# Softmax over 32,768 logits: loads and stores in units of 4 MB instead of 1 MB, with six large buffers and coarser compute pieces

## Chip, cores, metric

One core of one Trainium2 chip (trn2). The metric is the device time of one execution in microseconds (us). The median of the kernel before was 2552.28 us over 5 runs (2549.58 to 2561.99). The kernel before varied by half a per cent from run to run.

## The reference

```python
logits = np.random.randn(16, 256, 32768).astype(np.float32);  temperature = 1.0
scaled = logits / temperature
scaled = scaled - scaled.max(axis=-1, keepdims=True)
e = np.exp(scaled)
return e / e.sum(axis=-1, keepdims=True)
```

The input is 536.9 MB and so is the output: 1,073.7 MB have to cross between HBM (the large memory) and SBUF (the on-chip memory).

## The kernel before

Each row of 32,768 values is split in two halves, so the data becomes 8,192 rows of 16,384 values. A tile is 128 such rows (8.4 MB), and there are 64 tiles. Every piece of 2,048 columns is loaded, gets its own maximum (on DVE, the vector engine) and its own exponential and sum (on ACT, the scalar engine), and stays on chip. SP issues the loads and POOL (GpSimd) the stores; the DMA engines move the data. When all eight pieces of a tile are through, the local maxima and sums are combined into one factor per piece. Then every piece is scaled in place and stored.

```python
C = 2048                                    # columns of one piece; 8 KB per partition row
XBUFS = min((190 * 1024) // (C * 4), 4 * NCH)          # 23 buffers of 1 MB
...
for t in range(n_tiles):
    for c in range(NCH):                                # NCH = 8
        xc = xpool.tile([P, C], fp32, tag="x", name="xc")
        nc.sync.dma_start(out=xc[:rp], in_=x[r0:r1, bass.ts(c, C)])      # load, SP queue
        nc.vector.tensor_reduce(out=nm[:rp, c : c + 1], in_=xc[:rp], ..., op=A.max, negate=True)
        nc.scalar.activation(out=xc[:rp], in_=xc[:rp], func=Exp, bias=nm[:rp, c : c + 1],
                             scale=inv_t, accum_out=ssum[:rp, c : c + 1])
    with tc.high_priority():
        ...   # combine maxima (nM), ee = exp(nm - nM), S = sum(ee * ssum), f = ee / S
    for c in range(NCH):
        if scale_on_act(c):                             # c % 8 not in (1, 4, 7)
            nc.scalar.activation(out=xc[:rp], in_=xc[:rp], func=Copy, scale=f[:rp, c : c + 1])
        else:
            nc.vector.tensor_scalar_mul(out=xc[:rp], in0=xc[:rp], scalar1=f[:rp, c : c + 1])
        nc.gpsimd.dma_start(out=o[r0:r1, bass.ts(c, C)], in_=xc[:rp])    # store, POOL queue
```

The order of the instructions on each engine is not the order of this text: a scheduler fixes it when the kernel is built.

Of the kernel before, what the change touches and what calls it, by code (L numbers as in the profile page):

```python
# [1 line left out]

# [4 lines left out]


@with_exitstack  # L10
def kernel(
    ctx: ExitStack,
    tc: tile.TileContext,
    logits: bass.AP,
    temperature: bass.AP,
    out: bass.AP,
):
    nc = tc.nc

    inv_t = 1.0 / float(temperature)  # L20

    P = nc.NUM_PARTITIONS
    xf = logits.flatten_outer_dims()
    of = out.flatten_outer_dims()
    N, V = xf.shape

    SPLIT = 2 if (V % 2 == 0 and (N * 2) % P == 0) else 1
    C = 2048
    while (V // SPLIT) % C != 0:
        C //= 2  # L30
    x = xf.rearrange("n (h v) -> (n h) v", h=SPLIT) if SPLIT > 1 else xf
    o = of.rearrange("n (h v) -> (n h) v", h=SPLIT) if SPLIT > 1 else of
    NR, VR = x.shape
    NCH = VR // C
    n_tiles = (NR + P - 1) // P

    XBUFS = min((190 * 1024) // (C * 4), 4 * NCH)

    def scale_on_act(c: int) -> bool:
        return (c % 8) not in (1, 4, 7)  # L40

    xpool = ctx.enter_context(tc.tile_pool(name="x", bufs=XBUFS))
    spool = ctx.enter_context(tc.tile_pool(name="stats", bufs=4))

    fp32 = mybir.dt.float32
    Exp = mybir.ActivationFunctionType.Exp
    Copy = mybir.ActivationFunctionType.Copy
    X = mybir.AxisListType.X
    A = mybir.AluOpType

    swap_mask = [i ^ 1 for i in range(32)]

    for t in range(n_tiles):
        r0 = t * P
        r1 = min(r0 + P, NR)
        rp = r1 - r0

        nm = spool.tile([P, NCH], fp32, tag="nm", name="nm")
        ssum = spool.tile([P, NCH], fp32, tag="ssum", name="ssum")
        ee = spool.tile([P, NCH], fp32, tag="ee", name="ee")  # L60
        f = spool.tile([P, NCH], fp32, tag="f", name="f")
        ttj = spool.tile([P, NCH], fp32, tag="ttj", name="ttj")
        nMh = spool.tile([P, 1], fp32, tag="nMh", name="nMh")
        nMp = spool.tile([P, 1], fp32, tag="nMp", name="nMp")
        nM = spool.tile([P, 1], fp32, tag="nM", name="nM")
        Sh = spool.tile([P, 2], fp32, tag="Sh", name="Sh")
        Sp = spool.tile([P, 1], fp32, tag="Sp", name="Sp")
        rS = spool.tile([P, 1], fp32, tag="rS", name="rS")

        chunks = []  # L70
        for c in range(NCH):
            xc = xpool.tile([P, C], fp32, tag="x", name="xc")
            chunks.append(xc)
            nc.sync.dma_start(out=xc[:rp], in_=x[r0:r1, bass.ts(c, C)])  # L74
            nc.vector.tensor_reduce(  # L75
                out=nm[:rp, c : c + 1],
                in_=xc[:rp],
                axis=X,
                op=A.max,
                negate=True,  # L80
            )
            if inv_t != 1.0:
                nc.vector.tensor_scalar_mul(
                    out=nm[:rp, c : c + 1], in0=nm[:rp, c : c + 1], scalar1=inv_t
                )
            nc.scalar.activation(  # L86
                out=xc[:rp],
                in_=xc[:rp],
                func=Exp,
                bias=nm[:rp, c : c + 1],  # L90
                scale=inv_t,
                accum_out=ssum[:rp, c : c + 1],
            )

        with tc.high_priority():
            nc.vector.tensor_reduce(out=nMh[:rp], in_=nm[:rp], axis=X, op=A.min)  # L96
            if SPLIT == 2:
                nc.vector.stream_shuffle(out=nMp[:rp], in_=nMh[:rp], mask=swap_mask)  # L98
                nc.vector.tensor_tensor(  # L99
                    out=nM[:rp], in0=nMh[:rp], in1=nMp[:rp], op=A.min  # L100
                )
            else:
                nM = nMh
            nc.scalar.activation(  # L104
                out=ee[:rp], in_=nm[:rp], func=Exp, bias=nM[:rp], scale=-1.0
            )
            nc.vector.tensor_tensor_reduce(  # L107
                out=ttj[:rp],
                in0=ee[:rp],
                in1=ssum[:rp],  # L110
                scale=1.0,
                scalar=0.0,
                op0=A.mult,
                op1=A.add,
                accum_out=Sh[:rp, 0:1],
            )
            if SPLIT == 2:
                nc.vector.stream_shuffle(  # L118
                    out=Sh[:rp, 1:2], in_=Sh[:rp, 0:1], mask=swap_mask
                )  # L120
                nc.vector.tensor_tensor(  # L121
                    out=Sp[:rp], in0=Sh[:rp, 0:1], in1=Sh[:rp, 1:2], op=A.add
                )
            else:
                Sp = Sh[:, 0:1]
            nc.vector.reciprocal(out=rS[:rp], in_=Sp[:rp])  # L126
            nc.scalar.activation(  # L127
                out=f[:rp], in_=ee[:rp], func=Copy, scale=rS[:rp]
            )

        for c in range(NCH):
            xc = chunks[c]
            if scale_on_act(c):
                nc.scalar.activation(  # L134
                    out=xc[:rp], in_=xc[:rp], func=Copy, scale=f[:rp, c : c + 1]
                )
            else:
                nc.vector.tensor_scalar_mul(  # L138
                    out=xc[:rp], in0=xc[:rp], scalar1=f[:rp, c : c + 1]
                )  # L140
            nc.gpsimd.dma_start(out=o[r0:r1, bass.ts(c, C)], in_=xc[:rp])  # L141


# [1 line left out]
_INS = ['logits', 'temperature']  # L145
_OUTS = [((16, 256, 32768), 'float32')]
#: Inputs that are plain numbers.
_NUMBERS = {'temperature': 1.0}


# [26 lines left out]
```

## Time and profile before

| | before |
|---|---|
| median time | 2552.28 us |
| profiled span | 2554.0 us |
| busy: DMA / ACT / DVE | over 90% / 65% / 57% |
| rate in an undisturbed slice | 427 to 428 GB/s, read and written together |
| 1,073.7 MB at 427.5 GB/s | 2,512 us |

First, lines of the page of before. In part 2 each digit or number stands for one of 40 equal slices of the span (64 us each): the busy share of the DMA engines in tenths, and what they moved. Part 3 has one line per DMA queue (q1 carries the loads, q0 the stores): packets, MB, and the time their packets took as a share of 16 engines' span. Part 5 has busy us and mean ns, then the idle time before the group and who ended it. Part 6 has the median us from issue to landing at the end.

```profile
DMA  9999999999999999999999999999999999999997
GB/s 406 427 427 428 427 427 428 427 427 428 428 427 427 427 428 427 427 427 427 428 427 427 427 427 418 425 425 423 424 407 419 412 419 386 425 424 426 415 424 317
...
q1 hardware_dynamic: 73728, 536.90, 50.3%
q0 software_dynamic: 73728, 536.90, 50.0%
...
L75 DVE TENSOR_REDUCE nm<-xc 128x1 f32<-128x2048 f32 x512 | 1168.9, 2285 | 1037.7 <-DMA xc<-in_logits_dram 1037.7
...
xc<-in_logits_dram SPq DMA_DIRECT2D x512, 1024.0 KB, 26.4
out_dram<-xc POOLq DMA_DIRECT2D x512, 1024.0 KB, 24.8
```

The queues' shares add to 100%, and DVE waits 1,037.7 us for loads: the DMA engines bound the kernel. The rate is 427 GB/s for 24 slices, then it dips. A dip costs its shortfall: a slice of 64 us at 386 GB/s moves what about 58 us at 427.5 would, so it loses 6 us. Slices 25 to 39 lose about 21 us together, the last slice 16 us, the first 3 us.

A dip close up, as busy us of each engine in windows of 10 us (then DMA share and GB/s at the end), kernel before:

```profile
2100.00:2110.00 10.00, 5.16 (x9) 6.72 (x9) 0.00 (x0) 1.00 0.99 401
2110.00:2120.00 10.00, 8.42 (x7) 10.00 (x7) 5.37 (x8) 1.00 0.81 277
2120.00:2130.00 10.00, 4.40 (x2) 5.32 (x6) 0.00 (x0) 1.00 1.01 429
```

All eight stores of a tile are issued within the middle window (POOL, x8), and ACT is busy throughout it: data lay on chip while the DMA engines ran short of work.

### The profile page before, as it was taken

What the parts mean: (1) busy time and instruction counts of PE and PEld (TensorE: products, weight loads), DVE (VectorE), ACT (ScalarE), POOL (GpSimd) and SP (SyncE); (2) the same over time, 40 slices, a digit from 0 to 9 for tenths busy, and PEclk for the clock granted to TensorE, in tenths of its full rate; (3) what the DMA queues carried; (4) which work ended last, traced back from release to release, by engine and by line L of the source; (5) the groups of instructions that cost most, each with busy time, mean ns of one, the idle gap of its engine ahead of it and who ended that gap; (6) DMA issues with size and microseconds to landing.
All of it is one profiled execution on the core that took longest, in us unless ns stands there. A gap on an engine that the chain in (4) does not pass through costs nothing.

```text
span 2554.0 us, 5608 instructions
## 1 busy us (share of the span) xinstructions
DVE 1451.5 (57%) x1344; ACT 1663.9 (65%) x1473; POOL 344.1 (13%) x516
## 2 busy tenths in 40 slices
DVE  7565555556555555655655556555555555655551
ACT  7666756766666666765667566676575756666566
POOL 0111101111011110111101111011010101111011
DMA  9999999999999999999999999999999999999997
GB/s 406 427 427 428 427 427 428 427 427 428 428 427 427 427 428 427 427 427 427 428 427 427 427 427 418 425 425 423 424 407 419 412 419 386 425 424 426 415 424 317
DMA packets 147500, 1074.17 MB, mean 421 GB/s; under 512 B 16384, under 2 KB 16384, under 8 KB 16384
## 3 DMA queue, kind: packets, MB, share of 16 engines
q1 hardware_dynamic: 73728, 536.90, 50.3%
q0 software_dynamic: 73728, 536.90, 50.0%
q14 instruction: 44, 0.36, 0.0%
HBM read 536.87 MB, written 536.87 MB: 420 GB/s over the span
## 4 chain that ended last, share of the span: by engine, by line
issue 70%; DMA 28%; POOL 1%; DVE 0%; SPq 0%; ACT 0%; POOLq 0%
DMA out_dram<-xc 27%; DMA xc<-in_logits_dram 1%; POOL out_dram L141 1%; DVE nm L75 0%; SPq L74 0%; POOLq L141 0%; ACT xc L134 0%; ACT xc L86 0%; POOLq L172 0%; ACT f L127 0%; DVE nMh L96 0%; DVE nMp L98 0%; DVE nM L99 0%
## 5 line engine op out<-in xcount | busy, mean ns | idle before, releaser
L75 DVE TENSOR_REDUCE nm<-xc 128x1 f32<-128x2048 f32 x512 | 1168.9, 2285 | 1037.7 <-DMA xc<-in_logits_dram 1037.7
L86 ACT ACTIVATE xc<-xc,nm 128x2048 f32<-128x2048 f32 x512 | 1016.8, 1987 | 18.5 <-DVE nm L75 17.9
L141 POOL DMA_DIRECT2D out_dram<-xc x512 | 343.9, 677 | 2190.8 <-DVE xc L138 1668.8
L134 ACT ACTIVATE xc<-xc,f 128x2048 f32<-128x2048 f32 x320 | 612.2, 1987 | 0.1
L104 ACT ACTIVATE ee<-nm,nM 128x8 f32<-128x8 f32 x64 | 19.2, 300 | 556.1 <-DVE nM L99 556.1
L138 DVE TENSOR_SCALAR xc<-xc,f 128x2048 f32<-128x2048 f32 x192 | 235.7, 1279 | 1.8 <-ACT f L127 1.8
L127 ACT ACTIVATE f<-ee,rS 128x8 f32<-128x8 f32 x64 | 19.1, 298 | 289.6 <-DVE rS L126 289.6
L86 ACT ACTIVATION_READ_ACCUMULATOR xc<-xc,nm 128x1 f32 x512 | 95.6, 187 | 0.0
L107 DVE CUSTOM_DVE_ANT_0 ttj<-ee,ssum 128x8 f32<-128x8 f32 x64 | 10.0, 157 | 26.0 <-ACT xc L86 26.0
L126 DVE RECIPROCAL rS<-Sp 128x1 f32<-128x1 f32 x64 | 10.4, 163 | 1.9
L121 DVE TENSOR_TENSOR Sp<-Sh 128x1 f32<-128x1 f32 x64 | 10.2, 159 | 1.9
L96 DVE TENSOR_REDUCE nMh<-nm 128x1 f32<-128x8 f32 x64 | 10.1, 158 | 1.3
L99 DVE TENSOR_TENSOR nM<-nMh,nMp 128x1 f32<-128x1 f32 x64 | 10.0, 156 | 1.3
L98 DVE STREAM_SHUFFLE nMp<-nMh 128x1 f32<-128x1 f32 x64 | 9.7, 151 | 0.0
L118 DVE STREAM_SHUFFLE Sh<-Sh 128x1 f32<-128x1 f32 x64 | 9.7, 151 | 0.0
L107 DVE DVE_READ_ACCUMULATOR2_ANT Sh<- 128x1 f32 x64 | 5.3, 82 | 0.0
L86 ACT ACT_TABLE_LOAD x1 | 1.3, 1283 | 5.6 <-DMA xc<-in_logits_dram 5.6
L118 DVE LOAD_MASK_SELECT Sh<-Sh x64 | 0.9, 14 | 2.4
L98 DVE LOAD_MASK_SELECT nMp<-nMh x64 | 0.9, 14 | 2.0
L158 POOL MEMSET const-float32-0.0<- 128x1 f32 x1 | 0.1, 98 | 0.2 <-issue 0.2
L158 POOL MEMSET const-bfloat16-1.0<- 128x1 bf16 x1 | 0.1, 101 | 0.0
L158 POOL MEMSET const-float32-1.0<- 128x1 f32 x1 | 0.1, 98 | 0.0
(1 smaller groups left out, 0.1 us busy)
## 6 DMA issues: line engine op xcount, KB each, us to landing
xc<-in_logits_dram SPq DMA_DIRECT2D x512, 1024.0 KB, 26.4
out_dram<-xc POOLq DMA_DIRECT2D x512, 1024.0 KB, 24.8
```

Source lines behind the costliest of these rows:

```text
L75: nc.vector.tensor_reduce(out=nm[:rp, c : c + 1], in_=xc[:rp], axis=X, op=A.max, negate=True,)
L86: nc.scalar.activation(out=xc[:rp], in_=xc[:rp], func=Exp, bias=nm[:rp, c : c + 1], scale=inv_t, accum_out=ssum[:rp, c : c + 1],)
L98: nc.vector.stream_shuffle(out=nMp[:rp], in_=nMh[:rp], mask=swap_mask)
L104: nc.scalar.activation(out=ee[:rp], in_=nm[:rp], func=Exp, bias=nM[:rp], scale=-1.0)
L107: nc.vector.tensor_tensor_reduce(out=ttj[:rp], in0=ee[:rp], in1=ssum[:rp], scale=1.0, scalar=0.0, op0=A.mult, op1=A.add, accum_out=Sh[:rp, ...
L118: nc.vector.stream_shuffle(out=Sh[:rp, 1:2], in_=Sh[:rp, 0:1], mask=swap_mask)
L121: nc.vector.tensor_tensor(out=Sp[:rp], in0=Sh[:rp, 0:1], in1=Sh[:rp, 1:2], op=A.add)
L126: nc.vector.reciprocal(out=rS[:rp], in_=Sp[:rp])
L127: nc.scalar.activation(out=f[:rp], in_=ee[:rp], func=Copy, scale=rS[:rp])
L134: nc.scalar.activation(out=xc[:rp], in_=xc[:rp], func=Copy, scale=f[:rp, c : c + 1])
L138: nc.vector.tensor_scalar_mul(out=xc[:rp], in0=xc[:rp], scalar1=f[:rp, c : c + 1])
L141: nc.gpsimd.dma_start(out=o[r0:r1, bass.ts(c, C)], in_=xc[:rp])
```

## The change

The intent is fewer, larger transfers. A load or a store now covers 8,192 columns (4 MB, 32 KB in one piece per partition row); compute runs on pieces of 4,096 columns inside such a buffer, called a slot below.

```diff
+_IC = 8192
+_CC = 4096
+_SBUF_KB = 192
+_SCALE_ON_DVE = {1, 4, 7}
...
-    XBUFS = min((190 * 1024) // (C * 4), 4 * NCH)
+    XBUFS = max(NDC + 2, (_SBUF_KB * 1024) // (IC * 4))      # 6 slots of 4 MB
...
-        for c in range(NCH):
-            xc = xpool.tile([P, C], fp32, tag="x", name="xc")
-            nc.sync.dma_start(out=xc[:rp], in_=x[r0:r1, bass.ts(c, C)])
-            nc.vector.tensor_reduce(...)
-            nc.scalar.activation(...)
+        for d0, dn in dchunks:                               # 2 per tile
+            xs = xpool.tile([P, IC], fp32, tag="x", name="xs")
+            nc.sync.dma_start(out=xs[:rp, :dn], in_=x[r0:r1, d0 : d0 + dn])
+            for g0, gn in chop(dn, CC):                      # 2 per slot
+                xc = xs[:rp, g0 : g0 + gn]
+                nc.vector.tensor_reduce(...)
+                nc.scalar.activation(...)
...
-            nc.gpsimd.dma_start(out=o[r0:r1, bass.ts(c, C)], in_=xc[:rp])
+            nc.gpsimd.dma_start(out=o[r0:r1, d0 : d0 + dn], in_=xs[:rp, :dn])
```

The rest (the combination written for any power-of-two split, more buffers for the small statistics) computes the same. With four pieces per tile, only one of four is scaled on DVE instead of three of eight.

More of the change, by code (lines that the diff above doesn't have):

```diff
@@ L5 @@
 import concourse.tile as tile
-from concourse import bass_utils, mybir
+from concourse import mybir
 from concourse._compat import with_exitstack
+_SPLIT = 2
+_IC = 8192
+_CC = 4096
+_SBUF_KB = 192
+_SCALE_ON_DVE = {1, 4, 7}
 @with_exitstack
@@ L25 @@
     N, V = xf.shape
-    SPLIT = 2 if (V % 2 == 0 and (N * 2) % P == 0) else 1
-    C = 2048
-    while (V // SPLIT) % C != 0:
-        C //= 2
+    SPLIT = _SPLIT
+    while SPLIT > 1 and (V % SPLIT or (N * SPLIT) % P or V // SPLIT < 512):
+        SPLIT //= 2
     x = xf.rearrange("n (h v) -> (n h) v", h=SPLIT) if SPLIT > 1 else xf
@@ L33, with chop @@
     NR, VR = x.shape
-    NCH = VR // C
     n_tiles = (NR + P - 1) // P
-    XBUFS = min((190 * 1024) // (C * 4), 4 * NCH)
-    def scale_on_act(c: int) -> bool:
-        return (c % 8) not in (1, 4, 7)
+    IC = min(_IC, VR)
+    CC = min(_CC, IC)
+    def chop(total: int, step: int) -> list[tuple[int, int]]:
+        return [(s, min(step, total - s)) for s in range(0, total, step)]
+    dchunks = chop(VR, IC)
+    NDC = len(dchunks)
+    NCH = len(chop(VR, CC))
+    XBUFS = max(NDC + 2, (_SBUF_KB * 1024) // (IC * 4))
     xpool = ctx.enter_context(tc.tile_pool(name="x", bufs=XBUFS))
-    spool = ctx.enter_context(tc.tile_pool(name="stats", bufs=4))
+    spool = ctx.enter_context(tc.tile_pool(name="stats", bufs=8))
     fp32 = mybir.dt.float32
@@ L49 @@
     A = mybir.AluOpType
-    swap_mask = [i ^ 1 for i in range(32)]
+    n_rounds = SPLIT.bit_length() - 1
     for t in range(n_tiles):
@@ L62 @@
         ttj = spool.tile([P, NCH], fp32, tag="ttj", name="ttj")
-        nMh = spool.tile([P, 1], fp32, tag="nMh", name="nMh")
-        nMp = spool.tile([P, 1], fp32, tag="nMp", name="nMp")
-        nM = spool.tile([P, 1], fp32, tag="nM", name="nM")
-        Sh = spool.tile([P, 2], fp32, tag="Sh", name="Sh")
-        Sp = spool.tile([P, 1], fp32, tag="Sp", name="Sp")
-        rS = spool.tile([P, 1], fp32, tag="rS", name="rS")
-        chunks = []
-        for c in range(NCH):
-            xc = xpool.tile([P, C], fp32, tag="x", name="xc")
-            chunks.append(xc)
-            nc.sync.dma_start(out=xc[:rp], in_=x[r0:r1, bass.ts(c, C)])
-            nc.vector.tensor_reduce(
-                out=nm[:rp, c : c + 1],
-                in_=xc[:rp],
-                axis=X,
-                op=A.max,
-                negate=True,
-            )
-            if inv_t != 1.0:
-                nc.vector.tensor_scalar_mul(
-                    out=nm[:rp, c : c + 1], in0=nm[:rp, c : c + 1], scalar1=inv_t
-                )
-            nc.scalar.activation(
-                out=xc[:rp],
-                in_=xc[:rp],
-                func=Exp,
-                bias=nm[:rp, c : c + 1],
-                scale=inv_t,
-                accum_out=ssum[:rp, c : c + 1],
-            )
@@ L95 @@
-        with tc.high_priority():
-            nc.vector.tensor_reduce(out=nMh[:rp], in_=nm[:rp], axis=X, op=A.min)
-            if SPLIT == 2:
-                nc.vector.stream_shuffle(out=nMp[:rp], in_=nMh[:rp], mask=swap_mask)
+        nMh = spool.tile([P, 1 + n_rounds], fp32, tag="nMh", name="nMh")
+        Sh = spool.tile([P, 1 + n_rounds], fp32, tag="Sh", name="Sh")
+        rS = spool.tile([P, 1], fp32, tag="rS", name="rS")
+        slots = []
+        c = 0
+        for d0, dn in dchunks:
+            xs = xpool.tile([P, IC], fp32, tag="x", name="xs")
+            slots.append(xs)
+            nc.sync.dma_start(out=xs[:rp, :dn], in_=x[r0:r1, d0 : d0 + dn])
+            for g0, gn in chop(dn, CC):
+                xc = xs[:rp, g0 : g0 + gn]
+                nc.vector.tensor_reduce(
+                    out=nm[:rp, c : c + 1], in_=xc, axis=X, op=A.max, negate=True
+                )
+                if inv_t != 1.0:
+                    nc.vector.tensor_scalar_mul(
+                        out=nm[:rp, c : c + 1], in0=nm[:rp, c : c + 1], scalar1=inv_t
+                    )
+                nc.scalar.activation(
+                    out=xc,
+                    in_=xc,
+                    func=Exp,
+                    bias=nm[:rp, c : c + 1],
+                    scale=inv_t,
+                    accum_out=ssum[:rp, c : c + 1],
+                )
+                c += 1
@@ L99 @@
+        with tc.high_priority():
+            nc.vector.tensor_reduce(out=nMh[:rp, 0:1], in_=nm[:rp], axis=X, op=A.min)
+            for j in range(n_rounds):
+                mask = [i ^ (1 << j) for i in range(32)]
+                nc.vector.stream_shuffle(
+                    out=nMh[:rp, j + 1 : j + 2], in_=nMh[:rp, j : j + 1], mask=mask
+                )
                 nc.vector.tensor_tensor(
-                    out=nM[:rp], in0=nMh[:rp], in1=nMp[:rp], op=A.min
-                )
-            else:
-                nM = nMh
+                    out=nMh[:rp, j + 1 : j + 2],
+                    in0=nMh[:rp, j : j + 1],
+                    in1=nMh[:rp, j + 1 : j + 2],
+                    op=A.min,
+                )
+            nM = nMh[:, n_rounds : n_rounds + 1]
@@ L116 @@
             )
-            if SPLIT == 2:
+            for j in range(n_rounds):
+                mask = [i ^ (1 << j) for i in range(32)]
                 nc.vector.stream_shuffle(
-                    out=Sh[:rp, 1:2], in_=Sh[:rp, 0:1], mask=swap_mask
+                    out=Sh[:rp, j + 1 : j + 2], in_=Sh[:rp, j : j + 1], mask=mask
                 )
                 nc.vector.tensor_tensor(
-                    out=Sp[:rp], in0=Sh[:rp, 0:1], in1=Sh[:rp, 1:2], op=A.add
-                )
-            else:
-                Sp = Sh[:, 0:1]
-            nc.vector.reciprocal(out=rS[:rp], in_=Sp[:rp])
-            nc.scalar.activation(
-                out=f[:rp], in_=ee[:rp], func=Copy, scale=rS[:rp]
-            )
-        for c in range(NCH):
-            xc = chunks[c]
-            if scale_on_act(c):
-                nc.scalar.activation(
-                    out=xc[:rp], in_=xc[:rp], func=Copy, scale=f[:rp, c : c + 1]
-                )
-            else:
-                nc.vector.tensor_scalar_mul(
-                    out=xc[:rp], in0=xc[:rp], scalar1=f[:rp, c : c + 1]
-                )
-            nc.gpsimd.dma_start(out=o[r0:r1, bass.ts(c, C)], in_=xc[:rp])
+                    out=Sh[:rp, j + 1 : j + 2],
+                    in0=Sh[:rp, j : j + 1],
+                    in1=Sh[:rp, j + 1 : j + 2],
+                    op=A.add,
+                )
+            nc.vector.reciprocal(out=rS[:rp], in_=Sh[:rp, n_rounds : n_rounds + 1])
+            nc.scalar.activation(out=f[:rp], in_=ee[:rp], func=Copy, scale=rS[:rp])
+        c = 0
+        for i, (d0, dn) in enumerate(dchunks):
+            xs = slots[i]
+            for g0, gn in chop(dn, CC):
+                xc = xs[:rp, g0 : g0 + gn]
+                if (c % 8) in _SCALE_ON_DVE:
+                    nc.vector.tensor_scalar_mul(
+                        out=xc, in0=xc, scalar1=f[:rp, c : c + 1]
+                    )
+                else:
+                    nc.scalar.activation(
+                        out=xc, in_=xc, func=Copy, scale=f[:rp, c : c + 1]
+                    )
+                c += 1
+            nc.gpsimd.dma_start(out=o[r0:r1, d0 : d0 + dn], in_=xs[:rp, :dn])
 _INS = ['logits', 'temperature']
```

## The prediction

> **What bounds it now.** The 16 DMA engines. The page's slices show DMA 9 throughout, and 427 to 428 GB/s in nearly all of the first 24 slices. It must move 1,073.7 MB (read plus written); at 427.5 GB/s that is 2,512 us of a span of 2,554. The remaining 42 us are start (406 GB/s in slice 1), tail (317 in slice 40; the window over the last 54 us has 311, worth 15 us), and about 21 us of dips in slices 25 to 39 (386 to 425 GB/s). DVE is busy 57% and ACT 65%, so per tile (39.3 us of DMA) ACT needs about 27 us and DVE about 23. In a dip (around 2,111 us, 277 GB/s) most buffers hold loaded data not yet stored.
>
> **What changes.** The arithmetic and the bytes are the same. (1) Loads and stores go from 512 each of 1 MB (8 KB per partition row) to 128 each of 4 MB (32 KB rows); (2) buffers go from 23 of 1 MB to 6 of 4 MB, that is 23 to 24 MB; (3) compute pieces go from 2,048 to 4,096 columns. From the groups (2,285 ns, 1,987 ns, 1,279 ns at 2,048 columns) I estimate 4.4, 3.8 and 2.4 us each. With four pieces only one in four is scaled on DVE, not three in eight: DVE falls to about 21 us per tile, ACT stays near 27. Not critical.
>
> **Where time can move.**
> - *Packet overhead.* In the queue table one queue's 65,536 data packets fill 50.0% of 16 engines' span, about 312 ns per 8 KB. The Trainium skill ("DMA: Bandwidth & Descriptors", Why small descriptors are slow; Where 436 GB/s comes from) gives a few fixed cycles per packet and a ceiling of 435 GB/s, that is 301 ns per 8 KB. If the gap between 427.5 and 435 is per packet, rows of 32 KB pay a quarter of it: about 433 GB/s, 2,480 us (estimate). If it is not, 427.5 stays. I give the gain 55%.
> - *Starvation.* Six coarse slots hold three tiles. In the new instruction order the DVE scale of a tile stands behind the first reduce of the next tile's second half, and the last ACT scale behind the next tile's rescaling exponential. So half one is stored about 7 us, half two about 16 us after the next tile's landing. With both queues at half rate (19.7 us per 4 MB) each slot lives about 66 + 39 = 105 us of the 118 us that six slots allow. I expect about 12 us of slack, so no steady bubbles, and the dips of the late slices gone.
> - *Ends.* The start stays about 3 us; the tail has about 3 to 8 us of idle DMA instead of 15.
>
> **Prediction.** With the packet gain 2,480 + 12 = 2,492; without it 2,512 + 15 = 2,527. Together 2508 us, range 2482 to 2545. Chances: faster by over 2% 0.42, within 2% 0.52, slower 0.06.
>
> **What would show it.** Slices at 432 to 434 GB/s and packet shares below 50% each: packet gain; 427: none. Dips: late slices flat means no starvation. Data packets should fall from 131,072 to 32,768; if larger rows are cut into smaller packets, the gain cannot come. Loads should land after 35-50 us, not 26, without cost.
>
> **What would make it wrong.** A slot held longer than I count, so that loads wait for stores and stores for landings at once (regular dips every 39 us; then 2,560 or more); the chip cutting rows into packets; or descriptor writing for stores blocked by the longer DVE scale.

## The result, and the profile after

The changed kernel took 2501.04 us (median of 8 runs, 2497.36 to 2506.14), the kernel before 2555.66 us in the 15 runs that it is compared with. The ratio is 0.9791, 95% interval 0.9775 to 0.9808: 2.1% faster, with the 2% line inside the interval. (A ratio is the mean time of one kernel's fast runs over that of the other's of the same rounds, so it is not quite the ratio of the medians quoted.)

The answering lines of the page of after (slices of 62.4 us):

```profile
DMA  9999999999999999999999999999999999999998
GB/s 412 427 431 436 431 435 431 434 432 433 435 431 436 431 435 430 435 432 433 435 431 436 431 434 431 434 432 433 435 431 436 431 435 431 435 432 434 434 432 349
...
q1 hardware_dynamic: 18432, 536.88, 49.9%
q0 software_dynamic: 18432, 536.88, 49.9%
...
L85 DVE TENSOR_REDUCE nm<-xs 128x1 f32<-128x4096 f32 x256 | 1124.5, 4415 | 1108.8 <-DMA xs<-in_logits_dram 1108.8
...
xs<-in_logits_dram SPq DMA_DIRECT2D x128, 4096.0 KB, 26.6
out_dram<-xs POOLq DMA_DIRECT2D x128, 4096.0 KB, 32.0
```

Two things changed. The plateau rose to 433 GB/s (a single slice wobbles by a few GB/s because packets are now 32 KB and are counted where they start). And there are no dips in slices 3 to 39. The kernel is still bound by the DMA engines; the number of bytes is the same.

One turn of the loop in the chain of waits of after (start us, duration us, what):

```profile
984.83 35.09 DMA out_dram<-xs
...
1019.97 26.59 DMA xs<-in_logits_dram
...
1050.93 2.36 DVE xs L149
...
1062.40 35.48 DMA out_dram<-xs
```

A store frees a slot and the next load fills it. When that load has landed (1,046.6 us), DVE makes its first reduce and then the scaling that stands behind it, that of the tile before; the first store of that tile is issued 7.2 us after the landing. The second, 15.8 us after the landing, also waits for the second reduce, the new maxima and an ACT pass behind them. A turn takes 77.6 us, which is two tile periods of 38.8 us. The loop doesn't set the pace: in source order, where this tie is gone, the plateau is the same 433 GB/s (experiment 7).

The tail of after, in windows (DMA share and GB/s last):

```profile
2430.00:2440.00 10.00, 3.76 (x7) 8.75 (x6) 0.00 (x0) 1.00 1.04 449
2440.00:2450.00 10.00, 6.02 (x2) 5.15 (x2) 0.00 (x0) 1.00 0.46 197
2450.00:2460.00 10.00, 5.46 (x6) 4.39 (x3) 0.73 (x2) 1.00 0.86 367
```

The last load lands at 2,444 us and the stores of the last tile but one are issued only from 2,451 us on. Meanwhile the DMA engines have little to do.

### The profile page after: what moved, and what is told of

The parts are those of the page before. It is cut to its first block, busy times and chain, and to the rows that moved or that the text cites. A ratio compares the mean times of both kernels' runs of the same rounds, so it can differ in the third digit from the quotient of the medians.

```text
span 2495.6 us, 2722 instructions
## 1 busy us (share of the span) xinstructions
DVE 1329.9 (53%) x960; ACT 1682.3 (67%) x833; POOL 68.3 (3%) x132
## 2 busy tenths in 40 slices
DMA packets 36885, 1073.93 MB, mean 430 GB/s; under 512 B 4096, under 2 KB 4096, under 8 KB 4096
## 4 chain that ended last, share of the span: by engine, by line
DMA 78%; issue 16%; DVE 4%; ACT 1%; POOL 1%; ACTq 0%; POOLq 0%; SPq 0%
DMA out_dram<-xs 44%; DMA xs<-in_logits_dram 34%; DVE xs L149 3%; DVE nm L85 1%; POOL out_dram L157 1%; ACT xs L153 0%; ACT xs L92 0%; ACTq L188 0%; POOLq L157 0%; SPq L82 0%; ACT f L141 0%; DVE rS L140 0%; DVE Sh L134 0%; DVE Sh L131 0%; DVE ttj L119 0%
## 5 line engine op out<-in xcount | busy, mean ns | idle before, releaser
L85 DVE TENSOR_REDUCE nm<-xs 128x1 f32<-128x4096 f32 x256 | 1124.5, 4415 | 1108.8 <-DMA xs<-in_logits_dram 1108.8
L92 ACT ACTIVATE xs<-xs,nm 128x4096 f32<-128x4096 f32 x256 | 946.2, 3696 | 103.0 <-DVE nm L85 103.0
L153 ACT ACTIVATE xs<-xs,f 128x4096 f32<-128x4096 f32 x192 | 702.2, 3692 | 0.1
L116 ACT ACTIVATE ee<-nm,nMh 128x4 f32<-128x4 f32 x64 | 19.0, 297 | 603.7 <-DVE nMh L109 603.7
L149 DVE TENSOR_SCALAR xs<-xs,f 128x4096 f32<-128x4096 f32 x64 | 150.1, 2345 | 4.8 <-ACT f L141 4.8
L157 POOL DMA_DIRECT2D out_dram<-xs x128 | 68.1, 532 | 2411.2 <-DVE xs L149 1795.0
L141 ACT ACTIVATE f<-ee,rS 128x4 f32<-128x4 f32 x64 | 19.0, 297 | 77.1 <-DVE rS L140 77.1
L92 ACT ACTIVATION_READ_ACCUMULATOR xs<-xs,nm 128x1 f32 x256 | 47.8, 187 | 0.0
L140 DVE RECIPROCAL rS<-Sh 128x1 f32<-128x1 f32 x64 | 10.5, 164 | 2.2
L134 DVE TENSOR_TENSOR Sh<-Sh 128x1 f32<-128x1 f32 x64 | 10.2, 159 | 2.2
## 6 DMA issues: line engine op xcount, KB each, us to landing
xs<-in_logits_dram SPq DMA_DIRECT2D x128, 4096.0 KB, 26.6
```

The costliest lines, as they stand in the source:

```text
L85: nc.vector.tensor_reduce(out=nm[:rp, c : c + 1], in_=xc, axis=X, op=A.max, negate=True)
L92: nc.scalar.activation(out=xc, in_=xc, func=Exp, bias=nm[:rp, c : c + 1], scale=inv_t, accum_out=ssum[:rp, c : c + 1],)
L116: nc.scalar.activation(out=ee[:rp], in_=nm[:rp], func=Exp, bias=nM[:rp], scale=-1.0)
L140: nc.vector.reciprocal(out=rS[:rp], in_=Sh[:rp, n_rounds : n_rounds + 1])
L141: nc.scalar.activation(out=f[:rp], in_=ee[:rp], func=Copy, scale=rS[:rp])
L149: nc.vector.tensor_scalar_mul(out=xc, in0=xc, scalar1=f[:rp, c : c + 1])
```

## Experiments

**Theories.** *Packets*: each row of a transfer costs a fixed part, so rows of 32 KB instead of 8 KB raise the plateau. Rivals: *number of DMAs* (issues and completions, not rows), *order and buffers* (the gain is the missing dips, which come from what the scheduler put where), and *coarser compute*. In the text, "plateau" is the mean rate of the window from 250 to 2,250 us.

### 1. Rows cut to 8 KB inside 4 MB transfers

```diff
-            xs = xpool.tile([P, IC], fp32, tag="x", name="xs")
-            nc.sync.dma_start(out=xs[:rp, :dn], in_=x[r0:r1, d0 : d0 + dn])
+            xp = xpool.tile([P, IC // 2048, 2048 + 8], fp32, tag="x", name="xs")   # gap of 32 B
+            xs = xp[:, :, :2048]
+            nc.sync.dma_start(out=xs[:rp],
+                in_=x[r0:r1, d0 : d0 + dn].rearrange("p (q w) -> p q w", w=2048))   # stores alike
```

> The changed kernel with its 4 MB DMAs, six slots and compute pieces kept, but each on-chip row cut by a gap of 32 bytes after every 2,048 columns, so that a DMA consists of 8 KB pieces again. Packet theory (the plateau rate is set by the length of one piece): the queue table shows 131,072 data packets, the plateau falls back to 427 to 428 GB/s, time near 2,512 + 16 = 2,528 us, ratio to the kernel before about 0.99. Rival, fewer and larger DMAs: plateau stays at 433 GB/s and time near 2,500 us, ratio 0.979. Rival, buffers and order only: flat slices, and whatever rate the kernel after has, so also near 2,500 us.

Measured: 2524.25 us (2523.89 to 2524.74), ratio 0.9873 (0.9853 to 0.9893). Page of the padded rows:

```profile
GB/s 409 428 428 428 428 428 428 428 428 428 428 428 428 428 428 428 428 428 428 428 428 428 428 428 428 428 428 428 428 428 428 428 428 428 428 428 428 428 428 352
...
q0 software_dynamic: 67584, 536.88, 50.3%
q1 hardware_dynamic: 67584, 536.88, 50.3%
```

The number of DMAs, the slots, the compute pieces and the tail are those of after, and only the row length is not. The plateau is back at 428 GB/s, yet flat. The order of the DVE and ACT instructions is the same in both traces, instruction by instruction. The gap itself isn't the cause: rows of 8 KB without a gap run at 427 GB/s (experiments 5 and 6). So the long rows are worth 23 us (2524 to 2501), and the flatness doesn't come from them.

### 2. Small DMAs into the same slots

```diff
-            nc.sync.dma_start(out=xs[:rp, :dn], in_=x[r0:r1, d0 : d0 + dn])
+            for q0 in range(0, dn, 2048):      # four loads of 1 MB; stores alike
+                nc.sync.dma_start(out=xs[:rp, q0 : q0 + 2048],
+                                  in_=x[r0:r1, d0 + q0 : d0 + q0 + 2048])
```

> The changed kernel with its slots of 4 MB and its compute pieces kept, but each slot filled by four DMAs of 1 MB and emptied by four (8 KB pieces, 1,024 DMAs in all). Packet theory: the same as the padded rows, plateau 427 to 428 GB/s, near 2,528 us; the number of DMAs adds nothing (within 5 us of the padded rows). Rival, number of DMAs: this one falls to the old rate while the padded rows keep the new one; then the two differ by about 30 us.

Measured: 2544.48 us (2543.46 to 2544.84), ratio 0.9951. This expectation failed: 20 us above the padded rows at the same row length. Page of the small DMAs:

```profile
GB/s 407 428 427 427 428 427 427 428 427 427 428 427 408 428 427 427 415 427 427 416 427 428 427 418 427 428 416 423 427 428 416 427 427 420 427 427 427 416 427 349
```

The rate is that of 8 KB rows, but dips appear from slice 13 on. The built order of DVE shows a difference too: with small DMAs the scheduler put the sum of a tile behind all four reduces of the next tile, in several tiles from tile 19 on (which is worked on in slice 13); in after and in the padded rows it stands behind two. So either the small DMAs or this order could be the cause. Experiments 5 and 6 tell these apart.

### 3. The DMA part of the change alone

```diff
-_CC = 4096
+_CC = 2048
```

> The DMA part of the change alone: 4 MB DMAs with 32 KB rows and six slots, but compute pieces of 2,048 columns as before (eight per tile, three of eight scaled on DVE). Packet theory: plateau 433 GB/s and time within 8 us of the changed kernel, 2,493 to 2,509 us. Rival, that the coarser compute pieces are part of the gain: clearly slower, 2,515 us or more.

Measured: 2500.8 us (2498.6 to 2500.98), ratio 0.9778. The time is as expected: by the whole time, the coarser compute pieces are worth nothing. But its plateau is 431 GB/s, with three slices from 403 to 421, and its last slice is better, 411 against 349; the two cancel. The three slices lie where DVE scales a tile a whole tile late (tiles 21, 22 and 41), so dips from the order occur with 4 MB DMAs too.

### 4. The new code with the old sizes

```diff
-_IC = 8192
-_CC = 4096
+_IC = 2048
+_CC = 2048      # 24 buffers of 1 MB
```

> The new code with the old sizes: 1 MB DMAs, pieces of 2,048 columns, 24 buffers in place of 23. Packet theory plus dips: plateau 427 to 428 GB/s, dips in the late slices as in the kernel before, 2,540 to 2,560 us, ratio 0.995 to 1.00. If the one buffer more or the rewritten code removes the dips, about 2,530 us, ratio 0.99.

Measured: 2550.16 us (2548.6 to 2551.43), ratio 0.9974. As expected: the rewritten code with one more buffer is worth about 6 us; it still dips, but from slice 30 on and not from 25. Its DVE order is that of the kernel before up to tile 59, so the later start probably comes from the one buffer more (see experiment 5).

### 5. The kernel before in the order of its source

Every DVE and ACT instruction was pinned behind the one before it on its engine, so a tile is summed and scaled before the next tile's first reduce. Nothing else was touched.

```diff
+    pin = tc.keep_in_program_order
...
-            nc.vector.tensor_reduce(...)
+            pin(nc.vector.tensor_reduce(...))      # and so for every DVE and ACT instruction
```

> The kernel before, with every DVE and ACT instruction pinned to the order in which the source writes it (all of a tile, its sums and its scaling, before the next tile's first piece); sizes, DMAs and the 23 buffers untouched. Order theory (the late dips come from sums and scalings that the scheduler put a whole tile later in tiles 35 to 47 and so let all buffers fill): dips gone, slices flat at 427 GB/s, about 2,512 + 15 = 2,527 us, ratio 0.99. Rival, dips belong to 1 MB DMAs as such (issuing, completions): no change, 2,550 to 2,560 us.

Measured: 2536.99 us (2534.85 to 2537.92), ratio 0.9923 (0.9908 to 0.9938). Page of before, pinned:

```profile
GB/s 407 427 427 427 427 427 427 427 427 427 428 427 427 427 427 427 427 427 427 427 428 427 427 427 427 427 427 427 427 427 428 427 427 427 427 427 427 427 427 305
```

Every dip is gone with 1 MB DMAs and 23 buffers. The dips of before were the scheduler's order, and they cost 20 us. This is how late the order stood at the dip shown above, from the DVE timeline of before (start us, us, what; lines between left out):

```profile
2095.51 0.16 DVE L96 TENSOR_REDUCE nMh<-nm 128x1 f32<-128x8 f32 x1
...
2100.32 0.16 DVE L107 CUSTOM_DVE_ANT_0 ttj<-ee,ssum 128x8 f32<-128x8 f32 x1
...
2110.19 3.67 DVE L138 TENSOR_SCALAR xc<-xc,f 128x2048 f32<-128x2048 f32 x3
```

The first line combines the maxima of tile 53, after all eight of its reduces. The second is the sum of tile 52, one reduce of tile 54 later, and the third the scaling of tile 52, another two reduces later: 11 pieces late. Counted through the trace, the lag grows: the scaling is 2 pieces late at tile 0, 8 (a whole tile) at tile 33 and 12 at tile 59. The dips begin at tile 39, where it is 9 late, with 23 buffers, and at tile 46, where it is 10 late, with the 24 buffers of experiment 4. In after and the padded rows the lag is three of four pieces at most, in every tile.

The time is 10 us above what I expected, mostly because the tail is longer than I assumed: the last slice has 305 GB/s, so it loses 18 us of its 63, the first slice loses 3, and I had allowed 15 for both. The rest is the plateau of 427 in place of 427.5 (3 us) and 2 us between the profiled span and the device time.

### 6. The small DMAs in source order

The same pinning on the kernel of experiment 2.

> The small DMAs in 4 MB slots (2,544 us, with dips from slice 13 on) with the same pinning. Order theory: dips gone, 427 GB/s flat, within 5 us of the padded rows (2,524 us). Rival, number of DMAs: stays at 2,544 us.

Measured: 2534.72 us (2534.03 to 2534.99), ratio 0.9914. The dips are gone here as well (every slice from 2 to 39 at 427 or 428). It isn't within 5 us of the padded rows, though; 10 us remain. By the packets of the two traces, 5 us of them have come when 1,050 of the 1,074 MB have been moved: the plateaus, read to a decimal, are 427.3 and 428.2 GB/s. The last 24 MB cost another 3 us (68 against 65 us), and 3 us more pass between the last packet and the end (4.9 against 1.8). So a quarter of the DMAs, at the same row length, is worth some 10 us with the ends in it, and 5 us by the rate. The last 24 MB can't be put down to the small DMAs: without the pinning (experiment 2) they took 63 us.

### 7. The changed kernel in source order

> The changed kernel with the same pinning. Both theories: its plateau is already full, so it stays at 433 GB/s; only the tail gains, because the last tile but one is no longer scaled behind the last landing: 2,490 to 2,501 us, at most 10 us better than the changed kernel. If the pinning itself costs compute time that matters, slower than 2,501 us.

Measured: 2492.75 us (2492.49 to 2492.89), ratio 0.9750 (0.9733 to 0.9768). As expected: plateau 433 GB/s as before the pinning, last slice 372 instead of 349. The medians differ by 8 us, but the profiled runs by 4.5, of which the last 24 MB account for 3.7: the profile of after is that of its fastest run, and the traces don't show where its slower ones (up to 2506 us) lose more. This is the fastest kernel together with that of experiment 9. Loads now take 33.0 us to land and stores 47.0 (median): scaled tiles leave earlier, so more transfers queue.

### 8. A finer last tile

The last tile alone, of the pinned kernel, in pieces of 2,048 columns for loads, compute and stores.

```diff
+        fine = t == n_tiles - 1
+        CC = 2048 if fine else min(_CC, IC)
...          # for the last tile: one load and one store of 1 MB per piece
```

> The pinned changed kernel with the last tile alone loaded, computed and stored in pieces of 2,048 columns (1 MB DMAs), so that less compute stands between the last landing and the last store. From the durations in the trace of after (4.4 us against 2.3 us per reduce, 3.7 against 2.0 per ACT pass): first store of the last tile about 9 us earlier than pinned alone; 2,480 to 2,492 us, ratio to the kernel before about 0.973.

Measured: 2504.2 us (2503.86 to 2504.31), ratio 0.9795: 11 us slower than without, a miss. The reduces of the last tile, from the timeline of this kernel (each starts when its 1 MB has landed):

```profile
2433.73 2.29 DVE L94 TENSOR_REDUCE nm<-xs 128x1 f32<-128x2048 f32 x1 [5.87 <-DMA xs<-in_logits_dram]
2445.92 2.29 DVE L94 TENSOR_REDUCE nm<-xs 128x1 f32<-128x2048 f32 x1 [9.90 <-DMA xs<-in_logits_dram]
2458.08 2.29 DVE L94 TENSOR_REDUCE nm<-xs 128x1 f32<-128x2048 f32 x1 [9.88 <-DMA xs<-in_logits_dram]
2463.01 2.29 DVE L94 TENSOR_REDUCE nm<-xs 128x1 f32<-128x2048 f32 x1 [2.64 <-DMA xs<-in_logits_dram]
2465.45 2.29 DVE L94 TENSOR_REDUCE nm<-xs 128x1 f32<-128x2048 f32 x1 [0.16 <-DMA xs<-in_logits_dram]
```

While stores with 32 KB rows are under way, 1 MB (1.049 MB in decimal units) lands every 12.2 us: 86 GB/s, one fifth of the total of 433. When the stores have ended, it lands every 2.4 us. If the two queues take turns packet by packet, a queue with packets of 8 KB beside one with 32 KB gets 8 / (8 + 32), that is one fifth. By these figures the small loads were starved by the large stores; experiments 9 and 10 test it.

### 9. The finer last tile, loaded in 4 MB again

```diff
-            # last tile: one load of 1 MB per piece
+            nc.sync.dma_start(out=xs[:rp, :dn], in_=x[r0:r1, d0 : d0 + dn])   # every tile
```

> The last tile computed and stored in pieces of 2,048 columns as in the fine tail (2,504 us), but loaded in 4 MB DMAs with 32 KB rows again. Theory (the two queues take turns packet by packet, so loads in 8 KB packets beside stores in 32 KB packets got one fifth of the bandwidth and came late): the loss goes and a little is gained over the pinned kernel (2,493 us): 2,485 to 2,493 us. Rival (small last stores or finer compute cost the time): stays near 2,504 us.

Measured: 2493.1 us (2492.87 to 2505.13, 4 runs, of which three were 2493 and one 2505), ratio 0.9765. The loss of experiment 8 is gone in three of the four runs, so it lay in the small loads; the fourth run is as slow as experiment 8, and nothing says why. Nothing was gained over the pinned kernel, though: finer compute and stores in the last tile alone don't pay.

### 10. Small load rows beside large store rows everywhere

Pinned; loads as in experiment 2, stores of 4 MB.

> The pinned changed kernel with all loads in 1 MB DMAs of 8 KB rows, stores left at 4 MB with 32 KB rows. Turn-by-packet theory: wherever both queues have work, loads get about 87 of 433 GB/s (1 MB lands per 12 us) and stores about 346; stores finish early and loads then run alone, so landings come in bursts: stores land in about half the time of the pinned kernel (47 us before), loads are slow, and the rate lies between 427 and 433 GB/s wherever the buffers do not run out; 2,495 to 2,530 us. Rival (the queues share by bytes): loads and stores at equal rates, even landings, about 2,505 us, no bursts.

Measured: 2562.37 us (2561.52 to 2565.92), ratio 1.0027, plateau 423 GB/s. Turn by packet is borne out: stores land after 18.0 us (47.0 in the pinned kernel), loads of 1 MB after 39.8. By the packets' queues, loads held 4.6 of the 16 engines on average while both queues were under way (8.1 in experiment 5, with equal rows). But both the rate and the time are worse than I allowed for: for 37% of the time from 250 to 2,250 us only loads were under way, and they then moved 414 GB/s, against 428 with both. Why is not shown; loads of 32 KB rows alone are not slow (experiment 12).

### 11. Rows of 16 KB

```diff
-_IC = 8192
+_IC = 4096      # 2 MB DMAs, 12 slots, pinned
```

> Half-way point: 2 MB DMAs with 16 KB rows, 12 slots, pinned order. Packet theory: if a row costs a fixed part and a part per byte, the plateaus at 8 KB (428.2 GB/s in the padded rows) and at 32 KB (433.3) put 16 KB at 431 to 432 GB/s; from 1,073.7 MB at 431.5 and 15 us of ends, 2,503 us, between 2,497 and 2,508. If instead only rows of 32 KB, or only 4 MB DMAs, have the gain: near 2,524 or more.

Measured: 2504.97 us (2504.78 to 2505.31), ratio 0.9800, plateau 431 GB/s:

```profile
GB/s 410 431 431 431 431 431 431 431 431 431 431 431 431 431 431 431 431 431 431 431 431 431 430 431 431 431 431 431 432 431 431 431 431 431 431 431 431 431 431 364
```

One of 16 engines therefore needs, per row, 8,192 B × 16 / 428 GB/s = 306 ns for 8 KB, 608 ns for 16 KB and 1,211 ns for 32 KB. The steps, 302 ns for 8 KB more and 603 ns for 16 KB more, are proportional to the bytes. A straight line through the three leaves about 4 to 5 ns per row and a limit of about 435 GB/s. (The DMAs are of 4, 2 and 4 MB here, so the middle point also has twice the DMAs.)

### 12. Five slots

```diff
-_SBUF_KB = 192
+_SBUF_KB = 160      # 5 slots of 4 MB
```

> The changed kernel with five slots of 4 MB in place of six, the scheduler free to order. My prediction counted a slot's life as about 105 us of the 118 us that six slots allow; five allow 98 us. If that count holds, buffers run out every tile: dips in every slice, 2,530 to 2,700 us. If there is more slack than counted (queues that were only long because there was room), it stays within 1% of 2,501 us.

Measured: 2560.68 us (2559.64 to 2561.93), ratio 1.0019. The rate is below 433 GB/s in nearly every slice, as the count said. Page of five slots:

```profile
DMA  9999999999999999999999999999999999999998
GB/s 410 434 418 417 418 427 425 420 423 419 426 420 422 418 416 425 428 424 418 419 424 423 422 419 419 428 426 424 415 419 422 423 426 419 421 423 426 422 419 345
```

The loss is small, 2.4% over six slots, and the DMA share stays at 9 tenths. One explanation would be that one queue alone is slower than two. In the profile of after, loads alone at the start land 4 MB every 10.0 us (the first reduces of the slots start at 12.81, 22.80, 32.87 and 42.78 us), that is 420 GB/s. But this slow start belongs to that one profile. In the pinned kernel the first two landings are 9.69 us apart, which is 433 GB/s:

```profile
12.76 8.75 DVE L86 TENSOR_REDUCE nm<-xs 128x1 f32<-128x4096 f32 x2 [12.76 <-DMA xs<-in_logits_dram]
22.45 8.74 DVE L86 TENSOR_REDUCE nm<-xs 128x1 f32<-128x4096 f32 x2 [0.95 <-DMA xs<-in_logits_dram]
```

And five slots itself shows where its time goes, in three windows (DMA share and GB/s last): by the packets' queues, loads alone are under way in the first, the change from loads to stores falls in the second, and stores alone are under way in the third.

```profile
989.00:1001.00 12.00, 7.21 (x7) 11.36 (x7) 0.00 (x0) 1.00 1.01 434
1001.00:1009.00 8.00, 7.89 (x7) 8.00 (x3) 1.06 (x2) 1.00 1.00 369
1009.00:1017.00 8.00, 7.96 (x6) 8.00 (x6) 0.00 (x0) 1.00 1.00 430
```

One queue alone has nearly the full rate here; the time is lost at the change. When buffers run short, loads and stores come one after the other instead of side by side: from 250 to 2,250 us loads were alone for 20% of the time and stores for 21%. At the change the first store packet of 15 of the 16 engines lasted 1.8 to 2.8 us, where 1.2 us is usual, and a slow packet counts as busy, so the DMA share doesn't show the loss. From 250 to 2,250 us the time of packets beyond the usual adds up to 2.4% of all packet time, as much as the loss. The scheduler also built another DVE order for five slots, so this run doesn't isolate their number.

## Why the prediction was right, and where it was off

**The bound: right.** The DMA engines limit both kernels; the size of the compute pieces makes no difference to the time (experiment 3).

**Packet overhead: right, and somewhat smaller than stated.** I gave 55% to a plateau of 433 GB/s and a data time of 2,480 us; both were measured. The Trainium skill ("DMA: Bandwidth & Descriptors", Why small descriptors are slow (HBM only)) gives about 3 cycles per packet, and its section Where 436 GB/s comes from a ceiling of 435.2 GB/s at 850 MHz. Three row lengths lie near both: 4 to 5 ns per row, where 3 such cycles are 3.5 ns (estimate), and a limit of about 435 GB/s. That a row here is one packet of the page is not shown. By itself the row length is worth 23 us (experiment 1), not the 32 us of the prediction (2,512 to 2,480); a part belongs to the smaller number of DMAs, which the prediction didn't list (428 against 427 GB/s at 8 KB rows, about 5 us, experiments 1 and 6). The packets fell to 32,768 data packets, as said (36,864 less 4,096 small ones).

**No starvation, dips gone: right in outcome, incomplete in cause.** I took the dips of before for full buffers. Buffers did fill, but because sums and scalings stood more than a tile late in the built order: the same buffers and DMAs show no dip in source order (experiment 5), and that is worth 20 us. The changed kernel has no dips because its sizes led the scheduler to another order, which the prediction had read rightly, without seeing that the lag of the old order grows; this was a matter of the build as much as of the transfer size, since the same slots with small DMAs brought dips back (experiment 2) and pinning removed them (experiment 6).

**Slot life and slack: the count was useful, but the landing times missed.** I expected 105 of 118 us per slot. Five slots, with 98 us, do lose time in nearly every slice (experiment 12), so the slack seems to be less than one slot (their DVE order differs too). The time for which a slot holds its data was predicted well: stores about 7 and 16 us after the next tile's landing, measured 7.2 and 15.8. But I said that loads would land after 35 to 50 us, and they took 26.6. The failed step is "Loads should land after 35-50 us": I gave a store its 19.7 us at half rate and put all of the slack into waiting loads. The stores wait as well: they took 32.0 us (median; 35.1 in the loop shown), and the rest of the loop of 77.6 us is a load (26.6) and 16 us of compute. In source order, where stores don't wait for the next landing, loads take 33.0 us and stores 47.0.

**Ends: mis-sized.** I allowed 12 us beside the data time. The profiled run has 2,495.6 - 2,480 = 16 us. The last slice alone, 349 of 433 GB/s over 62.4 us, loses 12 us, where I had written 3 to 8 us of idle time for the tail. The DMA engines idle until the last tile but one is scaled, and that scaling stands behind the last landing's reduce. Pinning takes 8 us out by the medians, and 4.5 in the profiled runs (experiment 7).

**The sum.** 2508 us was the mean of two cases, 2,492 with the packet gain and 2,527 without. The first one happened, 9 us slower than said. That 2508 is only 7 us from the measured 2501.04 us is luck: it is a weighted mean that neither case gives. Whether the gain is over 2%, to which I gave 0.42, stays undecided, since the interval holds the 2% line.

| step | us, median | difference |
|---|---|---|
| before | 2556 | |
| before, source order | 2537 | 20 (in its own rounds): late sums and scalings |
| slots of 4 MB, DMAs of 1 MB, source order | 2535 | 2: slots and coarser compute |
| DMAs of 4 MB with rows of 8 KB | 2524 | 10: fewer DMAs, tail included |
| the changed kernel, rows of 32 KB | 2501 | 23: length of the rows |
| the changed kernel, source order | 2493 | 8: tail (3.7 in the profiled runs) and a part that no trace shows |

The fourth step also goes from a pinned to an unpinned kernel. Pinning was worth 8 us on the changed kernel, but it lengthened the last 24 MB of the small DMAs by 5 us (experiment 6). So the share of the number of DMAs alone is open beyond the 5 us of its rate; the padded rows in source order were not run.

## What to carry to other kernels

When a kernel is bound by transfers, look first at the flat part of its rate (row length sets it: here 428, 431 and 433 GB/s for 8, 16 and 32 KB), then at what falls below it: dips and ends are a matter of order and buffers, and together they were worth as much as the rows (20 and 8 us against 23). A static order can be read and pinned, and it should be compared whenever sizes change, because a size may win or lose through the order that it happens to produce. Keep loads and stores at the same row length and both always under way: small rows beside large ones get the smaller share, and with too few buffers the changes between loads and stores cost time (2.4% with five slots).

## What the Trainium skill lacked or had wrong

- "DMA: Bandwidth & Descriptors", Rules for kernel authors: it advises 1 MiB or more per DMA for bandwidth. With deep queues, rows of 32 KB in 4 MB DMAs moved 433 GB/s against 427 with 8 KB rows in 1 MB DMAs; of this, 428 to 433 is the row length and 427 to 428 the number of DMAs. The page compares sizes of a transfer, with which the rows grow too, but no row lengths at a fixed size of transfer on trn2.
- The same page, Queues, rings and completion order: it says that an engine takes turns between queues packet by packet, but not what follows for unequal rows. Loads with 8 KB rows beside stores with 32 KB rows got 86 of 433 GB/s, one fifth (1 MB per 12.2 us). These runs don't tell a turn of one row from a turn of an equal number of rows.
- No page says what a change from loads to stores costs when buffers are short. With five slots, 12 us of loads alone moved 434 GB/s and 8 us of stores alone 430, but the 8 us between them 369. Why is open.
- "SBUF — State Buffer", Summary: rules for kernel authors, says to estimate HBM transfers with about 358 GB/s. One core by itself, reading and writing, held 433 GB/s over 2,000 us. "HBM Reference" (Specifications) has about 425 for a core streaming alone, which is nearer.
- No page warns that in a kernel scheduled at build time a change of transfer size changes the instruction order, which here made up to 20 us of difference.
